# One small expert block at the end of the stream, router products in two column halves, POOL's subtraction in four pieces, and two rearrangements

## Chip, cores and metric

The kernel runs on one core of a Trainium2 chip. The metric is the device time of one execution in microseconds (us). Five engines work side by side and are ordered by semaphores: PE (TensorE, matrix products; PEld is its weight load), DVE (VectorE), ACT (ScalarE), POOL (GpSimd) and SP (SyncE), which here issues the DMA transfers from memory.

## Reference

Two layers over 512 tokens of width 1024 in fp32. The text below is cut to the parts that the change touches.

```python
for i in range(DEPTH):
    h = rms_norm(x, norm_mix[i])
    q, k, v, cu, cg, ga, gb = split(h @ w_in[i])
    y_a = dilated_mixture_attention(q, k, v) @ w_attn_out[i]
    y_b = conformer_conv(cu, cg, ...) @ w_conv_out[i] + b_conv_out[i]
    x = x + (sigmoid(ga) * y_a + sigmoid(gb) * y_b) @ w_out[i]
    h2 = rms_norm(x, norm_ffn[i])
    lg = h2 @ w_route_group + b          # 4 groups
    le = h2 @ w_route_expert + b         # 4 x 8 experts
    # top-1 group, then top-2 experts in it; gate = softmax(lg)[group] * softmax(top 2)
    for e in experts:                    # 32, each token goes to two of them
        y_e = (silu(h2[e] @ w_gate[e]) * (h2[e] @ w_up[e])) @ w_down[e]
    x = x + sum(gate_e * y_e)
    g_ple = sigmoid(rms_norm(x, norm_ple[i]) @ w_ple_gate[i])
    x = x + g_ple * (p[i] @ w_ple_proj[i])
return rms_norm(x, norm_final)
```

The routing makes 36 logits for a token (4 groups and 32 experts). An expert has three matrices of 1024 x 512.

## The kernel before

**Tiling.** The tokens are four tiles of 128 (`t` = 0 to 3), the width is eight slices of 128 (`k`). x stays in SBUF. Working tiles come from slots of a fixed number: `s4` has 45 of 128x1024 fp32 (512 KB), `s2` 16 of 128x512, `ps` the 8 banks of PSUM. Who asks for a slot that isn't free waits.

**Dense weights** come as chunks of 512 KB (`s_raw`, SP, L216), in the order `SEQ_CHUNKS`: v0–v3, then cu, cg, q, k, ga, gb, later `ao`, `wo`, `pe`, `pg`. Each is split into a high part (`s_hi`, ACT L234) and a low part (`s_lo`, L239; POOL alone for most chunks, for the first four and pg1–pg3 POOL takes one half and DVE the other, L237). A product of two split operands is three instructions, `mm3` L312 to L314. `self.look` and `self.ahead` say how many chunks ahead of the one in use are loaded and split.

**Start** (`run`). SP loads x[0], the identity, the gains, then for each t x[t] and a chunk. For each token tile `prep` makes the RMS, `s_n` = x times RMS times gain (on DVE) and puts the transposes (`split_T`, L419 on PE) on a list `todo`; the loop takes the first entry off the list at t = 1 and the second at t = 2, and calls `split_chunks(t)`. The mixer then begins with the products of V, `tokens_b`: for each token 8 k of three instructions; after each token one more entry of `todo` is taken.

**Routing** (`route_tile`, a generator that is advanced step by step between the dense products of `wo`). For a tile: transposes of x on PE (L832), eight fp32 products with the 36 router columns into one PSUM bank (L841), a copy of the logits on ACT (L868), a transpose of the 36 rows (L873), and then a chain of tiny DVE operations on 4 to 36 columns (L881 to L924) that finds group, experts and slots. `xh` (ACT, L859) and `xl` = x − xh (POOL, L860, 128x1024 in one instruction) are the split token tile, from which one-hot products (`gather_part`, `ps_xg`) later gather the rows of each expert.

**Experts** (`moe`). The 32 experts fill 28 slots that are ordered by the number of their tokens (`order_experts`) and 4 that are static (`NST`). Blocks of 128 rows: a pair holds two experts of 64 rows, a small block four of 32. `BLK` (L34) lists the 14 blocks: two static pairs, the two small blocks (the eight experts with the fewest tokens), ten pairs. Seven chunks `c` take two blocks each: gather of the next chunk's rows, gate and up products (`gate_up`, `ps_g` and `ps_u`, L102 in the trace), `hidden`, `down` of the blocks two before (`ps_y`), transposes, and `combine` (`ps_c`, added to x by DVE at L1150). After the loop come the load of the eight `pg` chunks, `down` of the last two blocks and their `combine`. An expert's weights are 12 items of 512 KB (gate, up, down, four each; 384 items in a layer). `self.items` holds them in the order in which they are used, and `pump` (L252) issues the next one on SP as soon as a slot of `s4` is free; `item_free` frees an item's slot after its last product. The overflow loop at L1292 stands in chunk `OVC` = 2, the `pe` products in chunk 4.

**PLE.** While the last `combine` runs token by token, `then(t)` transposes x (L1266), splits it, and starts the first half of the gate products (`first`, `ps_tb`) of the token before. After all tokens the RMS of each is made (two squares on ACT L384, a chain of DVE operations L392 to L401), and in `ple` the first half of each token is finished by `gated` (tanh on ACT L1412, two DVE operations L1414 and L1416 into x); then the second half follows token by token, with the next layer's `prep` behind it (`s_n`, L431).

Of the kernel before, what the change touches and what calls it, by code (L numbers as in the profile page):

```python
# [8 lines left out]
F32 = mybir.dt.float32  # L9
# [3 lines left out]
AF = mybir.ActivationFunctionType  # L13
OP = mybir.AluOpType
# [3 lines left out]
T, D, P = 512, 1024, 128  # L18
NT = T // P
KD = D // P  # L20
H, HD = 8, 64
CW, CK = 512, 31
NG, NPG, NE = 4, 8, 32
# [3 lines left out]
CAP = 64  # L27
GS = 256


NST, NSM = 4, 8
NDY = NE - NST
LD = 4
BLK = ([(2 * i, 2 * i + 1) for i in range(NST // 2)]  # L34
       + [tuple(range(NST + 4 * i, NST + 4 * i + 4)) for i in range(NSM // 4)]
       + [(i, i + 1) for i in range(NST + NSM, NE, 2)])
NB = len(BLK)


C_ID, C_ONE, C_BASE, C_PRIO, C_SLOT, C_IOTA = 0, 128, 256, 288, 320, 336  # L40
# [39 lines left out]
AH = 4  # L80
LK = 5, 3
# [82 lines left out]
class Trunk:  # L164
# [196 lines left out]
                self.done(c)  # L361
        return ps

    def tokens_b(self, cs, src, then):
        for c in cs:
            self.take(c)
        for t in range(NT):
            then(t, self.token_b(cs, src, t))


    def rsqrt(self, y, a, t, steps=3):
# [63 lines left out]
    def run(self):  # L435
        nc = self.nc
        self.layer = 0
        self.lim = NCH - 1
        nc.sync.dma_start(self.x[0], self.dr["x"][0:P])
        nc.sync.dma_start(self.ident, self.dr["cst"][:, C_ID:C_ID + P])  # L440
        gain = self.gain_row(0)
        for t in range(NT):
            if t:
                nc.sync.dma_start(self.x[t], self.dr["x"][t * P:(t + 1) * P])
            self.load_chunks(t)
        self.small(0)
        self.load_chunks(5)
        self.load_c2()
        nc.sync.dma_start(self.c1[:, C_ID + P:], self.dr["cst"][:, C_ID + P:C_N1])
        self.oneb = self.one.tile([P, P], BF, name="oneb")  # L450
        nc.vector.memset(self.oneb, 1.0)
        self.hT = Rows(self.s4, KD, F32R, "hTh"), Rows(self.s4, KD, F32R, "hTl")
        self.todo = []
        self.nc = Engines(self.tc, ("v", "sc", "g"))
        for t in range(NT):
            n = self.s4.get(F32, "n")
            self.prep(t, gain, self.rms(t, n), n)
            if t in (1, 2):
                self.todo.pop(0)()
            self.split_chunks(t)  # L460
        self.nc = nc
        self.s4.free()
        for l in range(self.L):
            self.layer = l
            self.mixer(l)
            self.moe(l)
            self.ple(l)
# [23 lines left out]
    def mixer(self, l):  # L491
        nc = self.nc
        v, act = nc.vector, nc.scalar
        base = l * NCH
        self.look, self.ahead = LK[0], AH
        pos = self.pos = {s: base + i for i, s in enumerate(SEQ_CHUNKS)}
        self.lim = pos["wo7"]
        conv, attn, side = [], [], []
# [5 lines left out]
        def value(t, ps):  # L504
            act.activation(vt(t), ps, AF.Copy)
            self.ps.free()
            if self.todo:
                self.todo.pop(0)()
        self.tokens_b([pos[f"v{i}"] for i in range(4)], self.hT, value)

        if l:
            self.load_c2()
        self.scale_small(l)
# [232 lines left out]
        for j in range(8):  # L746
# [14 lines left out]
            for h in range(2):  # L761
                a = slice(256 * h, 256 * h + 256)
# [46 lines left out]
    def route_init(self):  # L809
        self.nh = [[None] * NT for _ in range(2)]  # L810
        self.lgw, self.Ew, self.lgT = (self.s2.get(F32, n) for n in ("lgw", "Ew", "lgT"))
        self.Mb = self.tn(128, "Mb", BF)
        self.spos8, self.base8, self.slots8 = (self.tn(2 * NT, n) for n in ("sp", "sb", "sl"))
        self.spos, self.base, self.slots = ([a[:, i * NT:(i + 1) * NT] for i in range(2)]
                                            for a in (self.spos8, self.base8, self.slots8))
        self.order = None
        self.rc = self.tn(4, "rc")
        self.posb = self.ps.get(F32, "pos")
        self.oh0 = self.s4.get(F32R, "OH")
        self.xg0 = []  # L820

    def route_tile(self, t):

        nc = self.nc
# [13 lines left out]
            self.ps.free()  # L838
        def logits(h):
            for k in range(4 * h, 4 * h + 4):  # L840
                pe.matmul(pl[0:36, 0:P], self.gwr[:, k * 36:(k + 1) * 36], nT[h][:, k % 4 * P:(k % 4 + 1) * P],  # L841
                          start=k == 0, stop=k == KD - 1)
            self.s2.free()
        transposes(0)
        for _ in range(3):
# [11 lines left out]

        hi, lo = self.s4.get(F32R, "xh"), self.s4.get(F32R, "xl")
        act.activation(hi, x, AF.Copy)  # L859
        nc.gpsimd.tensor_tensor(lo, x, hi.bitcast(F32), op=OP.subtract)  # L860
        self.s4.free()
        self.nh[0][t], self.nh[1][t] = hi, lo
        self.rms_of(t, *ss, r)
        for _ in range(LAGS[1]):
            yield
        logits(1)
        lgT = self.lgT[0:36, t * P:(t + 1) * P]
        act.activation(lgT, pl[0:36, 0:P], AF.Copy)  # L868
        self.ps.free()
        for _ in range(LAGS[2]):  # L870
            yield
        pl = self.ps.get(F32, "lg")
        pe.transpose(pl[:, 0:36], lgT, self.cc(C_ID, P)[0:36, 0:36])  # L873

        w = self.lgw[:, t * P:(t + 1) * P]
        lg, G1 = w[:, 0:36], w[:, 40:44]
# [55 lines left out]
    def order_experts(self):  # L932

        v = self.nc.vector
        cnt = self.posb[:, 128:160]
        key, rank, small, base, self.cnt, top, rest, bs = (self.lgT[:, 32 * i:32 * i + 32] for i in range(8))
        bs, ss = bs[:, :8], bs[:, 8:16]
        over = lambda a, n: a.unsqueeze(1).to_broadcast([P, n, 32])
        down = lambda a, n: a.unsqueeze(2).to_broadcast([P, n, 32])

        v.scalar_tensor_tensor(key, cnt, -32.0, self.cc(C_KEY, 32), op0=OP.mult, op1=OP.add)  # L941
        src = key
        for i in range(0, NE, 8):
            v.max(out=top[:, i:i + 8], in_=src)
            if i + 8 < NE:
                v.match_replace(out=rest, in_to_replace=top[:, i:i + 8], in_values=src, imm_value=-1e9)
                src = rest
        oi = self.tn(NDY, "oi", I32)
        v.tensor_copy(oi, top[:, :NDY])
        v.tensor_scalar(oi, oi, 31, None, op0=OP.bitwise_and)  # L950
        self.order, self.order_v = oi, {}
        tmp = self.s2.get(F32, "ord")
        t3 = tmp.bitcast(BF).rearrange("p (a b) -> p a b", b=32)
        v.tensor_tensor(t3, over(key, 32), down(key, 32), op=OP.is_gt)
        v.tensor_reduce(rank, t3, axis=AX.X, op=OP.add)

        v.tensor_scalar(small, rank, float(NSM), 32.0, op0=OP.is_lt, op1=OP.mult)
        v.scalar_tensor_tensor(base, rank, float(NSM - 1), small, op0=OP.subtract, op1=OP.mult)
        v.scalar_tensor_tensor(base, rank, float(CAP), base, op0=OP.mult, op1=OP.subtract)
        if CAP * NST != CAP // 2 * NSM:  # L960
            v.tensor_scalar(base, base, float(CAP * NST - CAP // 2 * NSM), None, op0=OP.add)
        v.tensor_copy(base[:, :NST], self.cc(C_BASE, NST))
        v.tensor_add(self.cnt, cnt, small)
        self.ps.free()
        E8 = self.Ew[:, 0:256].rearrange("p (g e) -> p g e", e=32)
        t8 = tmp[:, 0:256].rearrange("p (g e) -> p g e", e=32)
        for o, a in ((ss, small), (bs, base)):
            v.tensor_tensor(t8, E8, over(a, 8), op=OP.mult)
            v.tensor_reduce(o, t8, axis=AX.X, op=OP.add)
        v.tensor_add(self.spos8, self.spos8, ss)  # L970
        v.tensor_scalar(ss, self.spos8, float(CAP), 4096.0, op0=OP.is_ge, op1=OP.mult)
        v.tensor_add(ss, ss, bs)
        v.tensor_add(self.slots8, self.spos8, ss)
        self.s2.free()
# [58 lines left out]
    def moe(self, l):  # L1033
# [217 lines left out]
        self.rh = []  # L1251
        self.src = [lambda k, a, b, s=s: s[a // P][:, k * P:(k + 1) * P] for s in gT]
        cs = [self.pos[f"pg{i}"] for i in range(4)]
        self.pg = []

        def first(t):
            self.pg.append(self.token_b(cs, self.src, t))

        def then(t):
            if t == NT - 1:  # L1260
# [9 lines left out]
            split_after(PGS[t + 1])  # L1270
            self.gT[0].append(hi)
            self.gT[1].append(lo)
            if t:
                first(t - 1)
        combine((NB - 2, NB - 1), then)
        first(NT - 1)
        for t in range(NT):
            junk = self.s4.get(F32, "j")
            r = self.rms(t, junk)
            self.s4.free()  # L1280
            h_ = self.tn(1, f"rh{t}")
            v.tensor_scalar(h_, r, 0.5, None, op0=OP.mult)
            self.rh.append(h_)


    def overflow(self, l):
# [113 lines left out]
            self.s4.used, self.s2.used, self.ps.used = was  # L1400


    def ple(self, l):
        nc = self.nc
        v, act = nc.vector, nc.scalar
# [1 line left out]
        self.look, self.ahead = 3, 1  # L1407
        last = l == self.L - 1

        def gated(t, h, ps):  # L1410
            th = self.s2.get(F32, "th")
            self.last = act.activation(th, ps, AF.Tanh, scale=self.rh[t]).ins  # L1412
            self.ps.free()
            v.scalar_tensor_tensor(th, th, 1.0, self.pp[h](t), op0=OP.add, op1=OP.mult)  # L1414
            xs = self.x[t][:, h * T:(h + 1) * T]
            self.last_v = v.tensor_add(xs, xs, th).ins  # L1416
            self.s2.free()

        for t in range(NT):
            gated(t, 0, self.pg[t])  # L1420
        self.pp[0].free()
        gain = self.gain_row(l + 1)
        if not last:
# [134 lines left out]
```

## Time and profile before

| what | value |
|---|---|
| median of 3 runs | 1818.47 us (1818.14 to 1821.3) |
| the profiled execution | 1818.76 us |
| its span from first to last instruction | 1817.0 us |
| outside the span (start and end of the execution) | 1.76 us |
| PE busy | 1720.2 us (95%) |
| DVE, ACT, POOL busy | 874.1, 540.2, 380.7 us |
| DMA | 478.66 MB, mean 263 GB/s |
| mean granted clock of PE | 0.986 |

A busy share is an average over stages with different limits. The span has in each layer a dense stage (0 to some 400 us and 930 to 1290), the experts (to 852 and 1746) and PLE. The experts' stage moves 384 items of 512 KB, the dense stages a few tens of chunks. The rows further down are named by line of the code, engine and tile: `s_w<-wdn` is the transfer of an expert's down weights into an item's slot.

### The profile page before, as it was taken

What the parts mean: (1) busy time and instruction counts of PE and PEld (TensorE: products, weight loads), DVE (VectorE), ACT (ScalarE), POOL (GpSimd) and SP (SyncE); (2) the same over time, 40 slices, a digit from 0 to 9 for tenths busy, and PEclk for the clock granted to TensorE, in tenths of its full rate; (3) what the DMA queues carried; (4) which work ended last, traced back from release to release, by engine and by line L of the source; (5) the groups of instructions that cost most, each with busy time, mean ns of one, the idle gap of its engine ahead of it and who ended that gap; (6) DMA issues with size and microseconds to landing.
All of it is one profiled execution on the core that took longest, in us unless ns stands there. A gap on an engine that the chain in (4) does not pass through costs nothing.

```text
span 1817.0 us, 24202 instructions
## 1 busy us (share of the span) xinstructions
PE 1720.2 (95%) x8324; PEld 1050.6 (58%) x8324; DVE 874.1 (48%) x2131; ACT 540.2 (30%) x1041; POOL 380.7 (21%) x203
## 2 busy tenths in 40 slices
PE   5999999998989999998999999998989899999997
PEld 4777787753244355444777777877514344355356
DVE  5688864572042243223648888537601332343146
ACT  4355534221011012103545554433201011022145
POOL 3445424300200001001444454252002000010021
PEclk9999999999999999999999999999999999999999
DMA  5222236389989999996242212564899899999931
GB/s 228 83 68 71 82 135 236 121 318 387 419 337 419 419 419 416 413 419 275 90 132 70 70 58 70 197 220 174 328 398 419 335 418 419 419 417 419 420 153 47
DMA packets 133616, 478.66 MB, mean 263 GB/s; under 512 B 14832, under 2 KB 15344, under 8 KB 133488
## 3 DMA queue, kind: packets, MB, share of 16 engines
q1 hardware_dynamic: 133488, 477.06, 67.5%
q8 instruction: 68, 1.11, 0.2%
q14 instruction: 60, 0.49, 0.1%
HBM read 474.90 MB, written 2.10 MB: 263 GB/s over the span
## 4 chain that ended last, share of the span: by engine, by line
PE 64%; DMA 20%; DVE 7%; issue 4%; ACT 2%; POOL 1%; SPq 0%; POOLq 0%; DVEq 0%; ACTq 0%
DMA s_w<-wdn 10%; PE ps_g L102 8%; PE ps_y L102 7%; DMA s_w<-wu 6%; PE ps_u L102 6%; PE ps_z L312 6%; PE ps_z L313 6%; PE ps_z L314 6%; PE ps_xg L102 5%; PE ps_c L102 5%; DMA s_w<-wg 3%; PE ps_tb L312 2%; PE ps_tb L313 2%; PE ps_tb L314 2%; PE ps_O L691 1%
## 5 line engine op out<-in xcount | busy, mean ns | idle before, releaser
L239 POOL TENSOR_TENSOR s_lo<-s_raw,s_hi 128x1024 fp32r<-128x1024 f32 x114 | 275.8, 2431 | 811.7 <-ACT s_hi L234 422.7
L102 PE MATMUL ps_u<-s_w,s_xg 128*64 128x512 f32 (+1 forms) x1024 | 240.1, 595 | 12.5 <-DMA s_w<-wu 12.1
L102 PE MATMUL ps_g<-s_w,s_xg 128*64 128x512 f32 (+1 forms) x1024 | 223.4, 603 | 14.2 <-DMA s_w<-wdn 9.3
L102 PE MATMUL ps_y<-s_w,s_hT 128*64 128x512 f32 (+1 forms) x1024 | 223.7, 601 | 11.3 <-DMA s_w<-wdn 10.7
L313 PE MATMUL ps_z<-s_hTl,s_hi 128*128 128x512 f32 x512 | 203.3, 397 | 0.0
L312 PE MATMUL ps_z<-s_hTh,s_hi 128*128 128x512 f32 x512 | 200.1, 391 | 0.0
L314 PE MATMUL ps_z<-s_hTh,s_lo 128*128 128x512 f32 x512 | 199.7, 390 | 0.0
L102 PEld LDWEIGHTS ps_u<-s_w,s_xg 128*64 128x64 f32 (+1 forms) x1024 | 67.7, 130 | 179.3 <-issue 117.3
L102 PEld LDWEIGHTS ps_y<-s_w,s_hT 128*64 128x64 f32 (+1 forms) x1024 | 69.6, 131 | 162.7 <-issue 113.8
L102 PEld LDWEIGHTS ps_g<-s_w,s_xg 128*64 128x64 f32 (+1 forms) x1024 | 64.8, 131 | 160.5 <-issue 127.6
L525 DVE SCALAR_TENSOR_TENSOR s_acc<-ps_z,smt,s_acc 128x511 f32<-128x511 f32 (+27 forms) x210 | 153.8, 732 | 4.6
L234 ACT ACTIVATE s_hi<-s_raw 128x1024 fp32r<-128x1024 f32 x120 | 125.5, 1057 | 8.6 <-PE ps_wo L313 4.2
L1105 DVE SCALAR_TENSOR_TENSOR s_h<-s_h,ps_g 128x512 f32<-128x512 f32 x28 | 19.2, 687 | 210.4 <-ACT s_h L1104 204.0
L1104 ACT ACTIVATE s_h<-ps_g,rs 128x512 f32<-128x512 f32 x28 | 19.2, 686 | 328.4 <-PE ps_g L102 287.7
L1150 DVE TENSOR_TENSOR s_x<-s_x,ps_c 128x512 f32<-128x512 f32 x112 | 75.2, 685 | 79.9 <-PE ps_c L102 47.4
L313 PEld LDWEIGHTS ps_z<-s_hTl,s_hi 128*128 128x128 f32 x512 | 96.2, 188 | 21.9 <-issue 3.1
L312 PEld LDWEIGHTS ps_z<-s_hTh,s_hi 128*128 128x128 f32 x512 | 96.1, 188 | 21.1 <-issue 1.0
L314 PEld LDWEIGHTS ps_z<-s_hTh,s_lo 128*128 128x128 f32 x512 | 96.2, 188 | 19.6 <-issue 0.8
L102 PE MATMUL ps_xg<-s_OH,s_xh 128*128 128x256 f32 x412 | 102.6, 290 | 3.7 <-DVE s_lgT L941 3.7
L1115 ACT ACTIVATE s_hT<-ps_hT 128x512 f32<-128x512 f32 x28 | 15.4, 596 | 300.3 <-PE ps_hT L102 300.3
L102 PE MATMUL ps_xg<-s_OH,s_xl 128*128 128x256 f32 x412 | 101.3, 286 | 0.0
L1106 DVE TENSOR_TENSOR s_h<-s_h,ps_u 128x512 f32<-128x512 f32 x28 | 19.3, 688 | 156.6 <-PE ps_u L102 156.6
(274 smaller groups left out, 2769.8 us busy)
## 6 DMA issues: line engine op xcount, KB each, us to landing
s_w<-wu SPq DMA_DIRECT2D x256, 512.0 KB, 9.9
s_w<-wdn SPq DMA_DIRECT2D x256, 512.0 KB, 9.9
s_w<-wg SPq DMA_DIRECT2D x248, 512.0 KB, 9.9
s_raw<-wd SPq DMA_DIRECT2D x124, 512.0 KB, 3.4
s_w<-wg SPq DMA_DIRECT2D x16, 256.0 KB, 7.4
s_x<-x SPq DMA_DIRECT2D x4, 512.0 KB, 9.9
out<-s_n SPq DMA_DIRECT2D x8, 256.0 KB, 2.0
s_gain<-gains SPq DMA_DIRECT2D x3, 512.0 KB, 3.8
```

What stands on the lines that cost most here:

```text
L102: i = f(*a, **k)
L234: nc.scalar.activation(hi, raw, AF.Copy)
L239: nc.gpsimd.tensor_tensor(lo, raw, hi.bitcast(F32), op=OP.subtract)
L312: mm(out, lh, rh, start=start, stop=False)
L313: mm(out, lh, rl, start=False, stop=False)
L314: mm(out, ll, rh, start=False, stop=stop)
L525: v.scalar_tensor_tensor(o, i, w, o, op0=OP.mult, op1=OP.add)
L691: nc.tensor.matmul(ps[64 * hh:64 * hh + 64, j * P:T], vt(j, (2 * p + hh) * HD, (2 * p + hh + 1) * HD), src, start=j == 0, stop=j == 3)
L1104: act.activation(t, pg, AF.Tanh, scale=rh[p])
L1105: v.scalar_tensor_tensor(t, t, 1.0, pg, op0=OP.add, op1=OP.mult)
L1106: v.tensor_mul(t, t, pu)
L1150: v.tensor_add(xs, xs, ps)
```

## The change

1. `BLK`: one of the two small blocks (the experts ranked 4 to 7) goes from fourth place to the last; the formula that gives each rank its base row is adapted by three more DVE operations on 32 columns.
2. Start: chunk 0 is split after the first token's preparation and that token's transposes are issued at once; chunks 1 and 2 are split after the second, chunk 3 after the third. In layer 0 the remaining transposes are issued in the middle of a token's V products (after 4 of 8 k) rather than behind each token, and chunks are split one ahead instead of four while V runs.
3. Routing: the products of even k go to columns 0 to 35, those of odd k to 64 to 99 of the array; two copies on ACT instead of one; the transpose becomes two accumulating products over 100 rows, which also add the two halves (rows between are set to zero once). POOL's subtraction for `xl` becomes four instructions of 256 columns.
4. PLE: each token's RMS is made in `then(t)`, and `gated(t, 0)` follows that token's first product at once.

```diff
-BLK = ([(2 * i, 2 * i + 1) for i in range(NST // 2)]
-       + [tuple(range(NST + 4 * i, NST + 4 * i + 4)) for i in range(NSM // 4)]
-       + [(i, i + 1) for i in range(NST + NSM, NE, 2)])
+BLK = ([(2 * i, 2 * i + 1) for i in range(NST // 2)] + [tuple(range(NST, NST + 4))]
+       + [(i, i + 1) for i in range(NST + NSM, NE, 2)] + [tuple(range(NST + 4, NST + NSM))])
...
-            self.load_chunks(t)
+            if t < 3:
+                self.load_chunks(t)
+        self.load_chunks(3)
...
-            if t in (1, 2):
+            self.split_chunks((0, 2, 3, 3)[t])
+            if t == 0:
                 self.todo.pop(0)()
-            self.split_chunks(t)
...
-        self.look, self.ahead = LK[0], AH
+        self.look, self.ahead = LK[0], AH if l else 1
...
-            if self.todo:
+            if l and self.todo:
                 self.todo.pop(0)()
-        self.tokens_b([pos[f"v{i}"] for i in range(4)], self.hT, value)
+        halves = []
+        def middle():
+            halves.append(0)
+            if not l and len(halves) % KD == KD // 2 and self.todo:
+                self.todo.pop(0)()
+        self.tokens_b([pos[f"v{i}"] for i in range(4)], self.hT, value, middle)
+        self.ahead = AH
...
+        self.nc.gpsimd.memset(self.lgT[32:64, :], 0.0)
...
-                pe.matmul(pl[0:36, 0:P], self.gwr[:, k * 36:(k + 1) * 36], nT[h][:, k % 4 * P:(k % 4 + 1) * P],
-                          start=k == 0, stop=k == KD - 1)
+                o = k % 2 * 64
+                pe.matmul(pl[o:o + 36, 0:P], self.gwr[:, k * 36:(k + 1) * 36], nT[h][:, k % 4 * P:(k % 4 + 1) * P],
+                          start=k < 2, stop=k >= KD - 2)
...
-        nc.gpsimd.tensor_tensor(lo, x, hi.bitcast(F32), op=OP.subtract)
+        for a in (slice(q, q + 256) for q in range(0, D, 256)):
+            nc.gpsimd.tensor_tensor(lo[:, a], x[:, a], hi[:, a].bitcast(F32), op=OP.subtract)
...
-        lgT = self.lgT[0:36, t * P:(t + 1) * P]
-        act.activation(lgT, pl[0:36, 0:P], AF.Copy)
+        halves = [slice(64 * i, 64 * i + 36) for i in range(2)]
+        lgT = self.lgT[:, t * P:(t + 1) * P]
+        for a in halves:
+            act.activation(lgT[a], pl[a, 0:P], AF.Copy)
...
-        pe.transpose(pl[:, 0:36], lgT, self.cc(C_ID, P)[0:36, 0:36])
+        for i, a in enumerate(halves):
+            pe.matmul(pl[:, 0:36], lgT[0:100], self.cc(C_ID, P)[0:100, a], start=i == 0, stop=i == 1)
...
         def first(t):
-            self.pg.append(self.token_b(cs, self.src, t))
+            self.gated(t, 0, self.token_b(cs, self.src, t))
...
+            junk = self.s2.get(F32, "j")
+            r = self.rms(t, junk)
...
+            self.rh.append(h_)
             if t:
                 first(t - 1)
```

## Rows read from the trace of the kernel before

**Rows 1.** Page, the chain that ended last: shares by engine, by line.
```profile
PE 64%; DMA 20%; DVE 7%; issue 4%; ACT 2%; POOL 1%; SPq 0%; POOLq 0%; DVEq 0%; ACTq 0%
DMA s_w<-wdn 10%; PE ps_g L102 8%; PE ps_y L102 7%; DMA s_w<-wu 6%; PE ps_u L102 6%; PE ps_z L312 6%; PE ps_z L313 6%; PE ps_z L314 6%; PE ps_xg L102 5%; PE ps_c L102 5%; DMA s_w<-wg 3%; PE ps_tb L312 2%; PE ps_tb L313 2%; PE ps_tb L314 2%; PE ps_O L691 1%
```

**Rows 2.** Windows: length, busy PE, PEld, DVE, ACT, POOL, clock, DMA share, GB/s.
```profile
430.00:510.00 80.00, 71.96 (x317) 22.24 (x315) 7.42 (x15) 7.00 (x15) 9.32 (x4) 1.00 1.03 417
510.00:540.00 30.00, 25.32 (x108) 11.21 (x108) 14.89 (x35) 1.01 (x2) 0.00 (x0) 0.94 0.82 298
540.00:720.00 180.00, 174.10 (x897) 84.28 (x894) 56.58 (x120) 27.75 (x54) 7.31 (x4) 1.00 1.03 419
```

**Rows 3.** Chain in order of time (start, us, what), both layers' experts.
```profile
475.06 9.87 DMA s_w<-wu
...
697.71 1.93 PE ps_y L102 x6
...
838.06 13.93 PE ps_y L102 x64
...
1732.38 13.94 PE ps_y L102 x64
```

**Rows 4.** Timeline of SP's issues at the end of each layer's experts.
```profile
820.17 10.31 SPq L252 DMA_DIRECT2D s_w<-wdn  x9
831.42 8.99 SPq L216 DMA_DIRECT2D s_raw<-wd  x8
...
1715.34 9.70 SPq L252 DMA_DIRECT2D s_w<-wdn  x8
```

**Rows 5.** DMA issues in 825 to 831: KB each, median us to landing.
```profile
s_w<-wdn SPq DMA_DIRECT2D x5, 512.0 KB, 9.9
```

**Rows 6.** Chain, pieces of PE: router, pair, gathers of two chunks, small block.
```profile
338.85 1.87 PE ps_lg L841 x16
...
379.76 7.02 PE ps_g L102 x32
...
700.66 7.67 PE ps_xg L102 x64
...
763.43 7.67 PE ps_xg L102 x64
...
1313.35 5.30 PE ps_g L102 x48
```

**Rows 7.** Chain of the first 90 us: first product of V, first behind V.
```profile
19.83 0.43 PE ps_tb L312
...
49.08 0.23 PE ps_z L313
```

**Rows 8.** Timeline of the first 70 us: POOL and DVE.
```profile
26.08 8.05 POOL L239 TENSOR_TENSOR s_lo<-s_raw,s_hi 128x1024 fp32r<-128x1024 f32 x3 [0.94 <-ACT s_hi L234]
...
31.86 2.83 DVE L102 TENSOR_TENSOR s_lo<-s_raw,s_hi 128x512 fp32r<-128x512 f32 x1
```

**Rows 9.** Waits of PE in the whole span: us in total, times, longest.
```profile
PE ps_tr L419 <- DVE s_n L102: 16.6, 3, 10.7
...
PE ps_tr L1266 <- DVE s_x L1150: 6.0, 6, 2.5
...
PE ps_tr L832 <- DVE s_x L852: 2.8, 2, 1.4
...
PE ps_tr L419 <- DVE s_n L431: 2.5, 2, 2.2
```

**Rows 10.** Timeline in layer 0's routing: DVE, then POOL.
```profile
368.34 2.38 DVE L884 SCALAR_TENSOR_TENSOR s_lgw<-s_lgw,c 128x4 f32<-128x4 f32 x1
...
368.34 2.37 POOL L860 TENSOR_TENSOR s_xl<-s_x,s_xh 128x1024 fp32r<-128x1024 f32 x1 [10.42 <-DVE s_lgw L883]
```

**Rows 11.** Timeline of DVE in layer 0's PLE.
```profile
894.35 0.68 DVE L1416 TENSOR_TENSOR s_x<-s_x,s_th 128x512 f32<-128x512 f32 x1
...
895.01 2.83 DVE L1414 SCALAR_TENSOR_TENSOR s_th<-s_th,s_pp 128x512 f32<-128x512 f32 x1
```

More of the change, by code (lines that the diff above doesn't have):

```diff
@@ L362, in token_b, with tokens_b @@
         return ps
-    def tokens_b(self, cs, src, then):
+    def tokens_b(self, cs, src, then, hook=None):
         for c in cs:
@@ L367, in tokens_b @@
         for t in range(NT):
-            then(t, self.token_b(cs, src, t))
+            then(t, self.token_b(cs, src, t, hook))
     def rsqrt(self, y, a, t, steps=3):
@@ L936, in order_experts @@
         key, rank, small, base, self.cnt, top, rest, bs = (self.lgT[:, 32 * i:32 * i + 32] for i in range(8))
+        bs32 = rest
         bs, ss = bs[:, :8], bs[:, 8:16]
@@ L957, in order_experts @@
         v.tensor_scalar(small, rank, float(NSM), 32.0, op0=OP.is_lt, op1=OP.mult)
-        v.scalar_tensor_tensor(base, rank, float(NSM - 1), small, op0=OP.subtract, op1=OP.mult)
+        v.tensor_scalar(bs32, rank, 4.0, -40.0, op0=OP.is_ge, op1=OP.mult)
+        v.scalar_tensor_tensor(bs32, bs32, -11.0, rank, op0=OP.add, op1=OP.add)
+        v.tensor_mul(base, bs32, small)
         v.scalar_tensor_tensor(base, rank, float(CAP), base, op0=OP.mult, op1=OP.subtract)
-        if CAP * NST != CAP // 2 * NSM:
-            v.tensor_scalar(base, base, float(CAP * NST - CAP // 2 * NSM), None, op0=OP.add)
+        v.tensor_scalar(base, base, -128.0, None, op0=OP.add)
         v.tensor_copy(base[:, :NST], self.cc(C_BASE, NST))
@@ L1253, in moe @@
         cs = [self.pos[f"pg{i}"] for i in range(4)]
-        self.pg = []
         def first(t):
-            self.pg.append(self.token_b(cs, self.src, t))
+            self.gated(t, 0, self.token_b(cs, self.src, t))
         def then(t):
@@ L1272, in then @@
             self.gT[1].append(lo)
+            junk = self.s2.get(F32, "j")
+            r = self.rms(t, junk)
+            self.s2.free()
+            h_ = self.tn(1, f"rh{t}")
+            v.tensor_scalar(h_, r, 0.5, None, op0=OP.mult)
+            self.rh.append(h_)
             if t:
@@ L1276, in moe @@
         first(NT - 1)
[L1277 to L1283, printed above, removed]
     def overflow(self, l):
@@ L1400, in overflow, with gated @@
             self.s4.used, self.s2.used, self.ps.used = was
+    def gated(self, t, h, ps):
+        nc = self.nc
+        th = self.s2.get(F32, "th")
+        self.last = nc.scalar.activation(th, ps, AF.Tanh, scale=self.rh[t]).ins
+        self.ps.free()
+        nc.vector.scalar_tensor_tensor(th, th, 1.0, self.pp[h](t), op0=OP.add, op1=OP.mult)
+        xs = self.x[t][:, h * T:(h + 1) * T]
+        self.last_v = nc.vector.tensor_add(xs, xs, th).ins
+        self.s2.free()
     def ple(self, l):
@@ L1408, in ple @@
         last = l == self.L - 1
[L1410 to L1420, printed above, removed]
+        gated = self.gated
         self.pp[0].free()
```

## Prediction

> **What bounds the kernel now.** I read the chain that ended last first: TensorE (PE) holds 64% of it, DMA 20%, and nearly all of the DMA is expert weights [rows 1]. So there are two kinds of stretch. The windows separate them. In the stage of the experts the DMA share is 1.03 at 417 to 419 GB/s, in 430–510 and 540–720 [rows 2]: one 512 KB item per 1.25 us, and PE is not what sets the pace there. Everywhere else PE does. The question for the stage of the experts is therefore when its last weight lands and how much PE work is left then. The chain answers it. Around the two small blocks it consists of landings (475.06, 9.87 us, one of six of about that length between 424 and 485), the last DMA wait of layer 0 is over by 697.71, and from there PE runs without a break to 838.06 + 13.93 = 852.0 [rows 3]. The issues of SyncE (SP) show that the last `wdn` was issued before 830.5 and the eight `pg` chunks behind it; with 9.9 us to landing [rows 5] the last expert weight is there by 840.4 [rows 4]. So 11.6 us of products follow the last weight. In layer 1 the same sum is 1746.3 − (1725.0 + 9.9) = 11.4 us [rows 3 to 5].
>
> **1. One small block goes to the end.** PE pays for a block by the instruction, four to an item: a pair has 32 for 8 items in 7.02 us (0.88 us per item), a small block 48 for 12 items in 5.30 us (0.44 per item), since four experts of 32 rows run in the four quadrants [rows 6]. DMA pays 1.25 us per item for either. Before, both blocks that are cheap for PE come early, PE is starved there, and the dear ones come last, where PE falls behind the landings. In a chunk PE has gate, up and down products, gathers and combinations: from gather to gather one chunk of two pairs takes it 763.43 − 700.66 = 62.8 us without a wait (part of that is the `pe` products, which only this chunk holds), for 48 items that take 60 us to land [rows 6]. It is nearly balanced, and the lag stays. With a small block in the last place its 48 items take 48 × 0.44 = 21 us of PE against 60 of DMA, so PE waits for each landing again. What follows the last landing is then one group of 16 quadrant instructions, 16 × 0.110 = 1.8 us (PE's piece after the last DMA wait of the chain is 1.93 [rows 3]). The last landing itself I leave where it is: the same 384 items at the same rate, and nothing that starts them moves.
> Gain: 11.6 − 1.8 = 9.8 in layer 0 and 11.4 − 1.8 = 9.6 in layer 1: **−19.5** rounded. The next things due are the `pg` chunks. They land behind the last `wdn`, 8 × 1.25 = 10 us, the first four by about 845.4. The first product that needs them comes one token's combination and transposes after `down`, and their splits on ACT (ScalarE) follow in the old order. I cost that at nothing; if it fails, the price is up to the 5 us to pg3's landing, and in the worst case the whole gain (rival 1). The three more tiny DVE (VectorE) operations of `order_experts` stand beside the stream of weights: nothing.
>
> **2. Start.** The products of V are 96 by 0.23, some 22 us, but run from 19.83 to 49.08, 29.3 us [rows 7]. PE waits three times for `s_n`, 16.6 us, the longest 10.7 [rows 9]; one of them is the start of the kernel. The rest is a queue on DVE: a `s_lo` of 512 columns takes 2.83 us at 31.86 while POOL (GpSimd) has three whole chunks in 8.05 us [rows 8]; an operation of that size takes 0.68 elsewhere [rows 11]. The change puts the splits of chunks 1 and 2 behind the second token's preparation, that of 3 behind the third's, all ahead of the fourth's, and puts the transposes of the next token inside a token's products, so PE has work while it waited before. Bounds: above, PE without any gap saves 29.3 − 22 = 7.3; below, half of the 2.1 us by which that `s_lo` was held, 1. I take **−4.5**: the products still share those 29 us with the transposes of three tokens, which are work and not waiting. The change in the order of the loads is none: x and chunks come out of SP in the same sequence. Nothing before layer 0 hides a gain there; the next product needs only PE and chunks that were split long before.
>
> **3. Route, four token tiles in each layer.** *Logits.* A tile's products with the router stand in the chain as 16 instructions in 1.87 us, 0.117 each [rows 6]. The change sends even and odd k to columns 0 to 35 and 64 to 99. No row shows products of 36 columns in two halves; the nearest are the expert blocks, where going from two parts of the array to four halves the time per instruction, 7.02/32 = 0.219 to 5.30/48 = 0.110 [rows 6]. So the gain lies between 0 and 0.94 us per tile, and I take 0.6, since the chunk of products comes in two pieces with a start of its own. Added: a second copy on ACT, and two products with 100 rows in place of a transpose with 36, at 0.117 for each pass of such a size 0.1 to 0.2 us more per tile.
> The rule that speaks against this: the Trainium skill, "TensorEngine Tiling (Array Packing)", Key Properties, says that a change of tiling mode, not just of tile, drains TensorE. By it alone the halves would cost a drain per group of logits; the kernel before has narrow column groups there too, so I count no difference.
> *POOL in four pieces.* DVE's operation of 4 columns at L884 takes 2.38 us where POOL runs its 2.37 from the same 368.34 [rows 10]. DVE is held until POOL's instruction ends. Four pieces of 256 columns, a quarter of 2.37 and some start each, 0.6 to 0.8 by my estimate, would let DVE in after at most 0.8 rather than 2.4. That DVE does get in between two POOL instructions is seen in the start: three chunks took 8.05, not 3 × 2.37 = 7.1 [rows 8]. Behind that chain of DVE stands PE's wait of 1.4 us for `s_x`, once per layer [rows 9]; at most the 1.6 us by which DVE is freed earlier is gained, at least nothing where PE has other products; I take 1.25 per layer. POOL itself gets up to 0.8 us longer per tile, beside PE's work.
> The Trainium skill, "SBUF — State Buffer", section "SBUF: two separate sides", calls the port pair that DVE and GpSimd share an exclusive lock, held for the whole instruction. The trace agrees, with 2.38 us for a 4-column operation. If the lock were taken again by the next piece, the pieces would be worth nothing (rival 3).
> Per layer: logits 4 × 0.6 = 2.4, pieces 1.25, second copy and products −0.15: 3.5. Bounds per layer: 0.6 slower (no halves, dearer extras) to 5 faster (3.75 + 1.6, less the extras). Two layers: **−7**.
>
> **4. PLE.** Before, the four RMS chains and all tanh steps stand after the combination; DVE has them in one heap, an operation of 0.68 us in it held to 2.83 [rows 11], and PE waits 2.2 us for the `s_n` of the next layer's first token [rows 9]. The change makes each token's RMS as soon as it is combined and its first gate half right after its product. Work is the same, so what it saves is the heap: 2.2 and a part of the 2.1 us of that held operation, 3 in all. Cost: two DVE operations of 0.68 us for a token [rows 11] now stand ahead of the adds of the next token, for which PE waits up to 2.5 us already [rows 9]: up to 1.4 us, twice a layer. In layer 1 the tail is PE from 1746 on, and only the last token's chain ends it, which stays: 0 there. I take **−3**, with bounds −5 and +3.
>
> **Sum.** −19.5 − 7 − 4.5 − 3 = −34.0 from the profiled execution's 1818.76, that is 1784.8; the median of the runs is 0.3 lower: **1784.5 us**. None of the four steps overlaps another: they lie in different stages, each PE-bound at its edge.
>
> **Rivals.**
> *1. The tail isn't given back* (0.17). The `pg` chunks or the first transposes become what is awaited after `down`, or the last landing comes later by what PE saves, because items are issued into slots that a lagging PE frees. For it: SP's issues are paced by free slots in some stretches. Against: the share of 1.03 in rows 2 says that landings are paced by DMA. Without the 19.5: 1804.
> *2. The start's edit is neutral*, since the work was placed early already (0.07): 1789.
> *3. DVE loses to POOL's next piece again* (0.10), so DVE's stall stays and only the logits gain: 1.25 less per layer, 1787.
> *4. Slower* (0.08): a gap of DMA opens in each chunk. While PE does gathers, combinations and hidden products it frees no slot; the windows around 510–540 had a share of 0.82 and 298 GB/s [rows 2], a loss of (418 − 298)/418 × 30 = 8.6 us, part of it the loop for the overflow. With the small block gone from the early part PE reaches these stretches with a fuller ring. If five chunks of each layer lose 4.2 us, that is +42 − 34, so 1826; it turns the result from 3.4 us per chunk on (34.0 / 10). Against it: 540–720, which is all pairs, held 1.03. I give half of it to a loss that just eats the gain.
> Forecast as stated: 0.58.
>
> **Range and chances.** A change under 0.2% (3.6 us) can't be told from none. Unknown costs: route −3 to +8, start −3 to +3.5, PLE −2 to +6, and the last landing ±5, by a part of the 8.6 us of rival 4's windows, which also can get shorter. All the lower ends together give 1772; the upper ends not all at once, and rival 1, 1804. So **1772 to 1804**. Faster 0.92 (forecast and rivals 1 to 3), same 0.04, slower 0.04.
>
> **What would show it.** Tail: in the chain of both layers landings of `wdn` up to about 840 (1735), then under 2 us of `ps_y`, then the combination. Start: V's last product at about 44.5, no wait of 10 us for `s_n`. Route: 16 logits in 1.2 to 1.5 us instead of 1.87, tiny DVE operations under 1 us where POOL runs, POOL's pieces near 0.70. PLE: no wait for `s_n` L431 of 2.2. Wrong it would be if the last `wdn` landed near 850 or if the DMA share fell under 0.95 in the pairs' chunks.

## The result

The changed kernel takes 1785.67 us (median of 4 runs, 1784.42 to 1789.39) against 1819.27 for the kernel before, measured beside it (1818.14 to 1821.3): a ratio of 0.9817, with 95% interval 0.98 to 0.9835. The forecast was 1784.5 in a range of 1772 to 1804. The time is right; two of its four terms are not, they miss in opposite directions, and the experiments show why.

The page of the changed kernel, its head and the chain that ended last by engine and line:

```profile
span 1782.6 us, 24295 instructions
PE 1697.5 (95%) x8348; PEld 1041.6 (58%) x8348; DVE 882.6 (50%) x2137; ACT 543.1 (30%) x1049; POOL 384.3 (22%) x229
PE 60%; DMA 23%; DVE 7%; issue 5%; ACT 2%; POOL 1%; SPq 0%; POOLq 0%; DVEq 0%; ACTq 0%
DMA s_w<-wdn 11%; DMA s_w<-wu 8%; PE ps_g L102 7%; PE ps_z L312 5%; PE ps_z L313 5%; PE ps_xg L102 5%; PE ps_z L314 5%; PE ps_y L102 5%; PE ps_u L102 5%; PE ps_c L102 4%; DMA s_w<-wg 3%; PE ps_tb L312 3%; PE ps_tb L314 3%; PE ps_tb L313 3%; DMA s_raw<-wd 1%
```

DMA's share of the chain rose from 20 to 23% [rows 1], and the share of `ps_y` fell from 7 to 5%: more of the path is landings, less is the work of PE behind them. The ends of both layers' experts in the chain of the changed kernel (start, us, what):

```profile
823.54 9.87 DMA s_w<-wdn
833.46 1.90 PE ps_y L102 x10
835.36 2.16 PE ps_c L1166 x8
...
1700.92 9.86 DMA s_w<-wdn
1710.84 7.89 DMA s_raw<-wd
1718.78 1.71 DVE s_lo L237
```

The last weight of layer 0 lands at 823.54 + 9.87 = 833.41, and 1.90 us of products follow. Before, the last one landed at 840.02 and 11.9 us followed, all within the unbroken 13.93 us of `ps_y` [rows 3]. In layer 1 the chain goes from the last `wdn` straight to the `pg` chunks and their split on DVE: that is what is late next.

Stage by stage, worked out from the first and last instructions of each kind in the traces (V: start to the first `ps_z`; routing: first `ps_wo` to first `ps_g`; experts: first `ps_g` to the last `ps_y`; PLE: from there to the next layer's first `ps_z`, or to the end):

| stage, us | before | changed | difference | forecast |
|---|---|---|---|---|
| V, layer 0 | 48.69 | 43.73 | −4.96 | −4.5 |
| routing 0, 1 | 73.99, 75.24 | 72.81, 72.93 | −1.18, −2.31 | −7 together |
| experts 0, 1 | 472.26, 472.26 | 461.45, 461.89 | −10.81, −10.37 | −19.5 together |
| PLE 0, end 1 | 89.77, 70.73 | 85.52, 69.92 | −4.25, −0.81 | −3 together |
| dense stages between | 257.01, 257.05 | 257.37, 257.02 | +0.33 | 0 |

The differences sum to −34.4, the difference of the spans. Routing of the kernel before is a bit longer as a rule than in this one trace: over the ten layers in five kernels that don't touch it, its median is 75.3, and over 14 layers with both edits 72.9. So its own worth is about −2.4 a layer.

The waits of PE over the whole span of the changed kernel (us in total, times, longest):

```profile
PE ps_tr L419 <- DVE s_n L102: 10.8, 2, 9.4
...
PE ps_tr L1283 <- DVE s_x L1169: 5.7, 6, 1.5
...
PE ps_tr L842 <- DVE s_x L863: 2.4, 2, 1.2
```

The wait for `s_n` L431 [rows 9] is gone; that of 16.6 us at the start is 10.8, of which 9.4 is the kernel's very beginning; the waits for x in PLE and in routing stayed nearly as long as they were.

### The profile page after: what moved, and what is told of

Read it like the earlier page. It is cut to its first block, busy times and chain, and to the rows that moved or that the text cites. A ratio compares the mean times of both kernels' runs of the same rounds, so it can differ in the third digit from the quotient of the medians.

```text
span 1782.6 us, 24295 instructions
## 1 busy us (share of the span) xinstructions
PE 1697.5 (95%) x8348; PEld 1041.6 (58%) x8348; DVE 882.6 (50%) x2137; ACT 543.1 (30%) x1049; POOL 384.3 (22%) x229
## 4 chain that ended last, share of the span: by engine, by line
PE 60%; DMA 23%; DVE 7%; issue 5%; ACT 2%; POOL 1%; SPq 0%; POOLq 0%; DVEq 0%; ACTq 0%
DMA s_w<-wdn 11%; DMA s_w<-wu 8%; PE ps_g L102 7%; PE ps_z L312 5%; PE ps_z L313 5%; PE ps_xg L102 5%; PE ps_z L314 5%; PE ps_y L102 5%; PE ps_u L102 5%; PE ps_c L102 4%; DMA s_w<-wg 3%; PE ps_tb L312 3%; PE ps_tb L314 3%; PE ps_tb L313 3%; DMA s_raw<-wd 1%
## 5 line engine op out<-in xcount | busy, mean ns | idle before, releaser
L102 PE MATMUL ps_g<-s_w,s_xg 128*64 128x512 f32 (+1 forms) x1024 | 207.4, 605 | 11.2 <-issue 6.3
L1169 DVE TENSOR_TENSOR s_x<-s_x,ps_c 128x512 f32<-128x512 f32 x112 | 75.2, 684 | 60.9 <-PE ps_c L102 47.2
```

The lines of the kernel that those rows point to most:

```text
L102: i = f(*a, **k)
L1169: v.tensor_add(xs, xs, ps)
```

## Experiments

Twelve runs, one of them of the changed kernel once more. "Part n" is the part of that number in the list of the change. The edits are cut to a few lines; what goes with them in the list of the change belongs to them here too.

**only_blk**: the kernel before with part 1 alone.

```diff
+BLK = ([(2 * i, 2 * i + 1) for i in range(NST // 2)] + [tuple(range(NST, NST + 4))]
+       + [(i, i + 1) for i in range(NST + NSM, NE, 2)] + [tuple(range(NST + 4, NST + NSM))])
```

> The kernel before with the new order of blocks alone (and its formula for base rows). Theory A, PE's lag behind the landings is given back: in each layer the last landing of wdn stays where it was relative to the start of the experts, and under 2 us of ps_y follow it instead of 11.5; the experts' stage is 10.5 us shorter in each layer, about 1798 us. Rival B, the gain at the end of the experts comes from the other edits (earlier start, earlier RMS): the stage is shorter by under 5 us, over 1809 us. Theory A says also what PLE does by itself: the pg chunks land 10 us after the last wdn now, so 1 to 3 us of the gain could come back there.

Measured: 1798.03 us, ratio 0.9883 (0.9869 to 0.9897). Experts 461.62 and 461.57, 10.7 shorter each; the last `wdn` lands at 841.13 and PE ends 2 us later; PLE 89.67, unchanged. Theory A, and without its addition: nothing comes back in PLE. The order of blocks explains the whole gain at the experts' end.

**only_start**: part 2 alone.

```diff
+            self.split_chunks((0, 2, 3, 3)[t])
+            if t == 0:
+                self.todo.pop(0)()
...
+        self.tokens_b([pos[f"v{i}"] for i in range(4)], self.hT, value, middle)
```

> The kernel before with the new order of splits and transposes of the start alone. Theory A, PE works on token 0 while the others are prepared: the first product behind V at 44.5 instead of 49.1, 4.5 us less, 1814 us. Rival B, the gain row landing earlier (7.9 instead of 9.2 us in the changed kernel) makes it: 1 to 1.5 us less where it lands early, nothing where it lands late.

Measured: 1814.17 us, ratio 0.9976 (0.9964 to 0.9987); V takes 43.13. Theory A. Rival B falls: over the seven kernels without the edit the gain row lands between 7.39 and 9.16 us and V lies between 47.70 and 49.09, over the seven with it the row lands between 7.91 and 9.16 and V lies between 43.13 and 45.35.

**only_half** and **only_piece**: the two edits of part 3, each alone.

```diff
+                o = k % 2 * 64
+                pe.matmul(pl[o:o + 36, 0:P], self.gwr[:, k * 36:(k + 1) * 36], nT[h][:, k % 4 * P:(k % 4 + 1) * P],
+                          start=k < 2, stop=k >= KD - 2)
```

> The kernel before with the router's products in two column halves alone. Theory A, the sixteen instructions take 1.0 us instead of 1.87, but most of it turns into waits of PE for the tiny operations of DVE and the copies of ACT: routing 0.5 to 1.5 us shorter per layer, 1 to 3 us in all. Rival B, as predicted: 0.6 per tile less the extras, 2.2 per layer, 4.5 in all. Rival C, a change of the array's layout drains it: no gain or a loss.

```diff
+        for a in (slice(q, q + 256) for q in range(0, D, 256)):
+            nc.gpsimd.tensor_tensor(lo[:, a], x[:, a], hi[:, a].bitcast(F32), op=OP.subtract)
```

> The kernel before with POOL's subtraction in four pieces alone. Theory A, DVE comes in between pieces: its tiny operations beside POOL take under 1 us instead of 1.6 to 2.4, and routing is 0.5 to 1.5 us shorter per layer. Rival B, POOL's next piece comes first again: the tiny operations still take over 2 us once in a tile, no gain. Rival C: DVE is freed, but PE doesn't wait for that operation, no gain.

Measured: halves alone 1819.59 us, ratio 1.0007 (0.9999 to 1.0016), routing 76.01 and 75.96, 0.7 longer than the median of the unmodified; pieces alone 1817.98, ratio 0.9989 (0.9978 to 1.0001), routing 74.84 and 74.92, 0.4 shorter. So neither gains alone what I gave it, and both lie within 0.3 us of the spread of the unmodified (73.97 to 75.76). Rival C of the halves (a drain) isn't the reason: its sixteen products do take 1.00 us instead of 1.87 [rows 6], as the chain of only_half shows:

```profile
338.52 1.00 PE ps_lg L843 x16
```

Summed over the routing of a layer, PE is busy 67.5 us in only_half (69.8 and 69.3 before), but idle for 8.6 (4.3 and 6.0 before): what the products give back, and more, is waited away. Where it goes is in the timelines of DVE, POOL and PE of only_half, in the third tile of layer 0:

```profile
354.30 2.37 DVE L907 TENSOR_TENSOR Mb<-s_Ew 128x32 bf16<-128x32 f32 x1
...
354.27 2.34 POOL L862 TENSOR_TENSOR s_xl<-s_x,s_xh 128x1024 fp32r<-128x1024 f32 x1 [6.85 <-ACT s_xh L861]
...
356.72 0.18 PE L922 MATMUL ps_pos<-Mb,trib 128*128 128x32 bf16 x1 [2.95 <-DVE Mb L907]
```

With faster products the tile's chain on DVE stands elsewhere when POOL begins. Here DVE's operation on 32 columns starts 0.03 us behind POOL's, is held for 2.37 us, and PE stands for 2.95 us waiting for its result; layer 1 has the same wait. With the pieces alone it is rival C: no tiny operation of DVE beside POOL takes over 0.71 us, yet PE is idle about as long as before, 5.2 us a layer against 4.3 and 6.0.

**route_both**: both edits of part 3 together, nothing else.

> Both edits of the routing, column halves and POOL in four pieces, nothing else. Theory A, each covers for the other: with halves alone DVE's chain runs into POOL's whole instruction at another place (2.38 and 2.24 us), with pieces alone PE isn't early enough; together routing is 1.2 to 2.4 us shorter per layer, 2.5 to 4.5 us in all. Rival B, the two add up as measured alone: +0.6 and -1.0, so -0.4 us. The clock of the last gathers (1.2 or 2.4 GHz level) moves each layer by up to 2.6 us either way in both.

Measured: 1813.07 us, ratio 0.997 (0.9959 to 0.998); routing 71.82 and 72.98. Theory A: −6 us by the medians (3.6 to 7.5 by the interval), where the two alone sum to −0.4. In the traces 4.4 of it are in routing, within what the theory said, and 2.1 in PLE, which the edits don't touch (for 1.6 of them only_rms below has the reason). The same place in the changed kernel, which has both:

```profile
349.46 0.73 DVE L917 TENSOR_TENSOR Mb<-s_Ew 128x32 bf16<-128x32 f32 x1
...
349.43 2.80 POOL L872 TENSOR_TENSOR s_xl<-s_x,s_xh 128x256 fp32r<-128x256 f32 x4 [6.27 <-issue]
...
350.25 0.18 PE L932 MATMUL ps_pos<-Mb,trib 128*128 128x32 bf16 x1 [1.32 <-DVE Mb L917]
```

The collision is the same, 0.03 us behind POOL's first piece. DVE is through after 0.73 instead of 2.37, and PE's wait falls by 1.63, from 2.95 to 1.32. The pieces make the halves pay.

**only_ple**: part 4 alone, and **only_rms**: of part 4 the early RMS alone, the first gate half stays behind the combination.

> The kernel before with the RMS of each token and the first gate half moved forward, alone. Theory A, the heap of DVE behind the combination is what PE waited for: PLE of layer 0 is 3 to 5 us shorter, the end of layer 1 about 0.7, some 1814 us. Rival B, the gain that PLE showed in the changed kernel (4.2 us in layer 0) comes from the earlier down products, since ACT splits pg while PE still works: under 1 us here. Rival C, DVE's adds come later behind the gate's two operations: slower by 1 to 3 us.

```diff
+            junk = self.s2.get(F32, "j")
+            r = self.rms(t, junk)
+            self.s2.free()
+            h_ = self.tn(1, f"rh{t}")
+            v.tensor_scalar(h_, r, 0.5, None, op0=OP.mult)
+            self.rh.append(h_)
             if t:
                 first(t - 1)
```

> The kernel before with only the RMS of each token moved into the combination; the first gate half stays behind it. Theory A, the heap is mostly the RMS chains (four of some 12 tiny operations and eight squares): 3 us or more of the 5 of both moves. Rival B, it is the gate's operations that are held by POOL (2.83 and 2.77 us): under 2 us here, the rest needs the gate moved too.

Measured: only_ple 1813.71 us, ratio 0.9975 (0.9963 to 0.9986), PLE 85.53 and 69.88: the whole gain of this stage is its own, theory A. only_rms 1810.17 us, ratio 0.9959 (0.9944 to 0.9974), PLE 82.97 and 68.02: theory A again, but it is not "3 us or more of the 5", it is 9.5 (6.80 + 2.71), and the early gate takes 4.4 of them back (2.56 + 1.86). The waits of PE in PLE of layer 0 with the RMS alone:

```profile
PE ps_tb L314 <- DVE s_gTl L1268: 0.8, 1, 0.8
PE ps_tr L1266 <- DVE s_x L1150: 0.3, 1, 0.3
PE ps_tr L1266 <- DVE rms L392: 0.3, 1, 0.3
```

1.4 us in place of 6.2 (3.0 for x, 2.5 for `s_n` and 0.7 for a low part). By the medians the whole kernel gains 6.5 us, by the interval of the ratio 4.7 to 10.2. The waits are 4.8 of the 6.8 us in layer 0. The other 2.0 are PE's own work: 83.4 us busy in the kernel before, 81.4 here, with the same products. The clock tells them apart. In the kernel before PE waits 2.5 us for x until 860.37, and then works at a mean granted clock of 0.54, that is mostly at the lower of its two levels (1.2 of 2.4 GHz); in all of only_rms's PLE it is 1.00 (windows of before, then of only_rms; columns as in [rows 2]):

```profile
860.00:863.50 3.50, 3.13 (x10) 2.65 (x11) 1.83 (x4) 3.47 (x5) 2.48 (x2) 0.54 0.00 0
```

```profile
851.20:934.10 82.90, 81.46 (x384) 66.29 (x385) 59.11 (x149) 51.86 (x101) 39.54 (x19) 1.00 0.31 104
```

The wait doesn't always bring the low clock. Five kernels with the old PLE have it there in layer 0 (89.64 to 89.87 us); route_both has the same wait without it, and 88.19.

With the gate moved too, PE waits 2.8 us for x, in place of 0.3. How, the timeline of DVE in the changed kernel shows:

```profile
853.12 2.71 DVE L1426 TENSOR_TENSOR s_x<-s_x,s_th 128x512 f32<-128x512 f32 x1
...
859.30 0.68 DVE L1169 TENSOR_TENSOR s_x<-s_x,ps_c 128x512 f32<-128x512 f32 x1
860.08 0.68 DVE L1424 SCALAR_TENSOR_TENSOR s_th<-s_th,s_pp 128x512 f32<-128x512 f32 x1
...
860.81 0.68 DVE L1426 TENSOR_TENSOR s_x<-s_x,s_th 128x512 f32<-128x512 f32 x1
...
861.47 0.68 DVE L1169 TENSOR_TENSOR s_x<-s_x,ps_c 128x512 f32<-128x512 f32 x1
```

The gate's two operations for token 1 (L1424, L1426) stand between the two additions of the last token (L1169), and PE's last transposes wait for the second one. An earlier one of them (853.12) was held by POOL to 2.71.

**place12** and **place10**: the changed kernel with its second small block as block 12 (a pair is last) or as block 10 (two pairs behind it).

```diff
+BLK.insert(12, tuple(range(NST + 4, NST + NSM)))
```

> The changed kernel with the second small block one place earlier: it is block 12, a pair is the last block. Theory A, what counts is that PE has caught up with the landings by the last chunk: 1.8 to 2.5 us of ps_y behind the last landing, time within 2 us of the changed kernel (1784 to 1788). Rival B, what follows the last landing is what the last block costs: a pair's down products again, 6 to 12 us behind it in each layer, 1795 to 1806 us.

> The changed kernel with the second small block as block 10, in the chunk that has the second half of the pe products; two pairs behind it in the last chunk. Theory A with the pe products (5.4 us in each of two chunks) as what makes PE late: PE catches up in this chunk, the last chunk takes it less than its landings, 2 to 3 us of products behind the last landing, 1784 to 1790 us. Rival A2, two pairs in the last chunk make PE late by themselves, with the last combinations in it: 8 to 12 us behind the last landing in each layer, 1799 to 1808 us.

Not shown in the edit are the two lines of the base rows' formula that the place needs; place10 has 10 for 12.

Measured: place12 1787.87 us, ratio 0.9831 (0.9815 to 0.9847), experts 462.39 and 461.74, with 2.0 us of products behind the last landing in both layers. Theory A: the kind of the last block doesn't matter. (Its PLE of layer 0 takes 87.11, 1.6 longer, at a mean granted clock of 0.98 instead of 1.00.) place10 1796.34, ratio 0.9872 (0.9855 to 0.989), experts 467.77 and 467.92: between A and A2, as half of the gain is lost. The timeline of PE in place10 and its chain at the end of layer 0 tell why:

```profile
813.50 1.93 PE L103 MATMUL ps_y<-s_w,s_hT 128*64 128x512 f32 x6 [0.18 <-DMA s_w<-wdn]
```

```profile
819.87 8.46 PE ps_c L103 x29
828.33 13.94 PE ps_y L103 x64
```

In the order of the program the combination of blocks 10 and 11 stands ahead of `down` of 12 and 13. It can't start before block 11's products are through and copied out. PE has caught up here: it takes block 11's last weights as they land, at 813.45, and is through with them by 815.5. With the copies by ACT and DVE it runs without a break only from 819.87. From there PE has 8.46 + 13.94 = 22.4 us and ends at 842.27; the last weight lands at 833.43. So 8.8 us of the old lag of 12 are made in the last chunk alone: two pairs leave 16 down items behind block 11's, 20 us of landings, against 28.8 us. A small block in that chunk makes it 24 items, 30 us, more than what PE has to do, since its down products cost PE no more than a pair's (16 × 0.44 = 7.0 us against 13.94 / 2). The other 3 us were there before the last chunk: in the kernel before, PE's unbroken run starts 9.5 us behind block 11's last landing (820.06, 829.6), in place10 6.4.

**again** and **gate_late**: the changed kernel once more, and with the first gate half of a token issued after the additions of the next one.

```diff
             if t:
                 first(t - 1)
+            if t > 1:
+                self.gated(t - 2, 0, pgs[t - 2])
```

> The changed kernel once more, unaltered, beside the next one: 1784 to 1787 us, stages within 0.5 us of the first trace save the start, where the landing of the gain row moves it by 1.3 us, and the last gathers of routing, whose clock moves them by up to 2.6 us.

> The changed kernel with the first gate half of a token issued after the next token's additions (gate of t-2 behind the product of t-1). Theory A, the two operations of the gate ahead of the second addition of token 3 are what PE waits for at the end of combine (1.07 and 1.51 us): 1 to 2 us less per layer in PLE and its counterpart in layer 1, 1782 to 1784 us. Rival B, the heap of DVE only moves behind the last product, where the next layer's s_n waits for it: PLE of layer 0 1 to 3 us longer, 1786 to 1788 us.

In gate_late `first` only makes the product and puts it into the list `pgs`.

Measured side by side: 1787.15 us (1785.08 to 1788.58) and 1783.07 (1782.05 to 1785.62). PLE 85.51 and 69.90 in the one, 84.50 and 68.94 in the other: theory A, 1.0 us in each layer. The two medians differ by more than these 2 us. The repeat's stages are as in the first trace, but for V (44.71 against 43.73), routing (71.75, 71.76 against 72.81, 72.93) and experts (1.5 and 0.6 longer, a miss of the 0.5 that I had allowed).

**gate_behind**: the changed kernel with all of the change but the early gate.

```diff
-            self.gated(t, 0, self.token_b(cs, self.src, t))
+            self.pg.append(self.token_b(cs, self.src, t))
...
+        for t in range(NT):
+            gated(t, 0, self.pg[t])
```

> The changed kernel with the first gate half left behind the combination, as in the kernel before, and all else of the change, the early RMS too. Theory A, the early gate costs what it cost beside the kernel before (85.53 against 82.97 us in layer 0's PLE, 69.88 against 68.02 behind layer 1's experts): 4.4 us less than the changed kernel, 1781 to 1783 us. Rival B, the loss is paid elsewhere here, since PLE begins with fewer splits of pg done: PLE of layer 0 over 84.5 us, 1784 to 1787 us.

Measured: 1781.04 us (1777.26 to 1783.09), ratio to the kernel before 0.9798 (0.9782 to 0.9815). PLE 82.93 and 67.45 against 85.52 and 69.92: theory A, 5.1 us less in the two stages. It is the fastest kernel of the study. Its lead over the changed kernel was measured in another series; what shows it is the stages in the traces, not a ratio of the two.

## Why the prediction was right, and where not

**The sum: partly luck.** Against the traces' −34.4 the forecast's −34.0 is near because its errors cancel: routing gave 3.5 us less than forecast, the tail 1.7, PLE 2.1 and the start 0.5 more.

**The tail: right.** Forecast −19.5, measured −21.2, from the place it named: landings to the end, then 1.90 us of `ps_y` (1.8 forecast). "The last landing itself I leave where it is" holds: measured from the first expert product it came 460.3 us in before and 459.5 in the changed kernel (layer 0). The reason I gave for the lag was only half of it. I compared a whole chunk (62.8 us against 60) and concluded that the lag stays; place10 shows that most of it is made new in the last chunk, by the order of the combination and `down` against 20 us of landings. Two of my readings hid this. PE does not run "without a break" from 697.71: the chain has ACT's and DVE's copies from 825.8 to 829.6, ahead of that combination, and PE is idle for 2.0 us of them. And the `pe` products are not in one chunk only: they stand in chunks 4 and 5 (715 to 721 and 778 to 784), so half of them lie in the 62.8 us.

**The start: right** within half a us; the edit alone gives it (only_start), whenever the gain row lands.

**Routing: the step that failed is the sum of two prices.** The logits were 0.6 per tile by forecast and are 0.87, so more. The two products in place of the transpose cost 0.22 more per tile (0.40 against 0.18 in the chains), near the forecast's 0.1 to 0.2; but I took 0.15 off once per layer instead of once per tile, and with that put right the sum was 3.05 per layer, not 3.5. The 1.25 for the pieces came from PE's wait of 1.4 us for `s_x` [rows 9], and that wait stayed (1.2). And I added the two prices as if PE set the pace. Part of PE's time turned into waits: in the changed kernel it waits for ACT's `s_nT` and `s_lgT`, 0.8 and 0.6 us a layer, and for DVE. Alone, the halves were worth nothing (+0.7 a layer), since DVE ran into POOL elsewhere; I had priced that stall where the old trace had it. Together they are worth 2.4 a layer by the medians of the traces. Rival 3 fell: held operations took at most 0.77 us beside the pieces. By the Trainium skill, "SBUF — State Buffer", section "SBUF: two separate sides", the shared port is locked for a whole instruction; the trace agrees, with 2.37 us beside one long instruction and 0.73 beside the first of four short ones.

**PLE: right only in its direction (−5.1 against −3, just past its bound of −5), wrong in both of its parts.** I took the saving as 3 and the cost of the gate as up to 1.4 us twice a layer, put none of that cost into the −3, and expected 0 in layer 1. The early RMS alone saves 9.5, 2.7 of it in layer 1, and the early gate costs 4.4. The saving was mis-sized twice over: I counted the wait for `s_n` and a held operation, and left out the wait of 2.5 us for x, which goes too, and the products at the lower clock behind it, 2.0 us in layer 0. The gate's cost lies where I had it, ahead of the next additions. I should have priced the two moves apart and asked for each; then the text would have said that half of this part is a loss.

**Rival 4** didn't occur. Windows of the changed kernel (length, busy PE, PEld, DVE, ACT, POOL, clock, DMA share, GB/s):

```profile
430.00:510.00 80.00, 73.01 (x334) 31.03 (x334) 21.96 (x48) 8.03 (x16) 9.34 (x4) 0.99 0.96 385
510.00:540.00 30.00, 29.84 (x159) 9.21 (x157) 2.04 (x5) 0.69 (x1) 0.00 (x0) 0.96 1.01 393
540.00:720.00 180.00, 176.73 (x884) 88.41 (x885) 62.94 (x134) 29.42 (x56) 7.32 (x4) 0.99 1.03 418
```

The gaps of DMA [rows 2] moved to the front and did not multiply: against 418 GB/s the first two windows lose 6.3 and 1.8 us, 8.1 together, where the second alone lost 8.6.

**Rival 1** is there in small. In layer 1 the chain runs through the `pg` chunks (7.89 us of landing and 1.71 of split). PE has transposes and combinations meanwhile; it waits 0.8 us in each layer for `s_gTl`, which DVE makes behind that split.

## To carry to other kernels

In a stream bound by DMA, count the landings that remain when the last long stretch of other work begins against that work; a block that is cheap for the engine belongs in that last stretch, whatever its place there. A gain on one engine of a chain of short steps is worth what the next engine leaves of it, and an edit that moves the chain in time may run into another stall: measure edits together and apart. When an edit moves two steps, price and try each, since the sum can hide that one of them is a loss. And look at the granted clock behind a wait of PE: in the kernel before, a wait of 2.5 us was followed by products at a lower clock, worth 2.0 us.

## What the runs showed of the hardware

- Products of 36 columns in two halves of the array run side by side: 16 instructions in 1.00 us instead of 1.87 (0.063 us each), although each uses only 36 of its 64 columns. The Trainium skill, "TensorEngine Tiling (Array Packing)", Key Properties, says that different tiles can execute in parallel, which agrees.
- Four POOL instructions of 128x256 take 2.80 us, one of 128x1024 took 2.37: 0.14 us for each further instruction. DVE gets in between two of them: after 0.73 us, not 2.37.
- How much of the last gathers runs at the lower granted clock (1.2 of 2.4 GHz) varies from run to run: 28 of their instructions took 3.58 us in layer 0 of the changed kernel (mean granted clock 0.92 in 364 to 374) and 5.08 in only_blk (0.72 in 370 to 382), with the same work and, in both, a wait of PE of 1.86 us just before them; this alone moves routing by over 1 us.
